# Block two's attention: a written TensorE order, raw queries and keys, one norm chain, compression between column tiles

## The chip, the core and the metric

One core of one Trainium2 chip runs the whole program. The metric is device time in microseconds, the median of several executions. TensorE does the matrix products, VectorE, ScalarE and GpSimd (POOL in the views) the elementwise work, and the SyncE queue (SP) issues the weight loads from HBM.

## What is computed

Two transformer blocks over 256 tokens of width 1024. The change is in the second. It normalises its input, projects it by one wide matrix and runs three branches: a sparse attention (NSA) with a compressed, a selected and a window part, a causal depthwise convolution of 31 taps, and an attention over a memory of 256 tokens. Each branch has an output product and a sigmoid gate of 1024 columns; their sum goes through another product, and a feed-forward layer follows.

```python
def hybrid_layer(x, mem, ...):
    proj = rms_norm_2(x, norm_mix) @ w_in
    q_nsa, kv_nsa, g_nsa, conv_in, q_mem, g_merge = split(proj)
    q = rms_norm_2(heads(q_nsa, 8), nsa_qk_norm[0])             # 8 heads of 64, 2 groups
    kc = rms_norm_2(compress_blocks(k_c, ...), nsa_qk_norm[1])  # gelu(blocks @ w1) @ w2
    vc = compress_blocks(v_c, ...)
    ks, kw = rms_norm_2(k_s, nsa_qk_norm[2]), rms_norm_2(k_w, nsa_qk_norm[3])
    o_nsa = gates of three softmax attentions: (kc, vc), (ks, v_s), (kw, v_w)
    u = a * sigmoid(ag)                                         # conv_in = a, ag
    br_conv = silu(layer_norm(conv31(u))) @ w_conv_out
    o_m = softmax(rms_norm(q_mem) @ rms_norm(km).T) @ vm        # 4 heads of 128
    merged = gm0 * (o_nsa @ w_nsa_out) + gm1 * br_conv + gm2 * (o_m @ w_mem_out)
    h = x + merged @ w_out
    ...
```

## The kernel before, in words

Activations lie with features on partitions and 256 tokens along the free axis. Big products take each fp32 weight tile as a high and a low half (fp32r): `Stream.prepare` loads 128x1024 fp32 (512 KB) into one of four `raw` buffers (L492), ScalarE writes the high half (L495) and VectorE, or POOL for the tiles listed in `pool`, the low half (L499); there are three buffers for each half. `gemm_b` then does, for each column tile of 128 columns and 8 slices of depth, 24 products: high by high (L318), high by low (L320), low by high (L322). Two column tiles share a PSUM bank, and an evacuation follows (L1039 for heads and convolution inputs, L1073 for gates).

`block_two` runs: the first 8 column tiles of `w2a` (compressed, selected and window keys, queries), a narrow product for the branch gates, the values (`w2v`, L358), the next 8 tiles (the convolution's two inputs), `compress` (chunks of `wc1`, L1174, loaded into eight of the 27 big tiles; a fold, L1180; the gelu; second products L1198 and L1213; a norm, L1203), the last 4 tiles (memory queries), then `nsa` and `mem_attention`. `head_norms` (L990 to L1001) takes squares, sums over the head by products (L996) and a chain of some twelve small VectorE steps (L371 to L377); it runs once for queries, once for keys and once for memory queries. Key norms are spread by products with the identity (L1231) and multiplied into the keys. In `nsa`, compressed scores (L1258) go through a softmax over 16 columns (L1260 to L1274) and are transposed (L1277); for each of eight heads `first(n)` makes scores (L1292), mask and maximum (L1298), exponentials (L1305) and the scaling by one over the sum and the gate (L1312, on POOL); `second(n)` transposes (L1324), copies (L1327) and multiplies by the values (L1334, L1335), adds the compressed part (L1337) and splits the result ("on", L416 and L417). A memory head does scores (L1362), maximum (L1364), exponentials (L1368), scaling (L1373), transposes (L1375), values (L1380) and the split ("om").

The program text gives each engine's instructions priorities, and a scheduler with its own model of costs turns them into a fixed order for each engine; weight loads and evacuations are raised. Only dependencies and this scheduler set TensorE's order. The 24 gate tiles (`w2g`) come after attention in the text, and the scheduler uses them to fill TensorE between attention's steps. The convolution's 124 taps (L1392, L1394) run on VectorE at low priority, followed by its norm (L1404 to L1427), which ends in "uc". After attention come three branch products, memory, NSA and convolution, in this order.

PSUM has eight banks: two "pj" for column tiles, three "pa", two "pb" for transposes and one "pc" for the heads' outputs.

Of the kernel before, what the change touches and what calls it, by code (L numbers as in the profile page):

```python
# [17 lines left out]
T = 256  # L18
# [54 lines left out]
def constants():  # L73
# [22 lines left out]
    c["half"] = (p[:, None] // 64 == np.arange(2)[None]).astype(f)  # L96
    c["mean64"] = (p[:, None] // 64 == p[None] // 64).astype(f) / 64
# [17 lines left out]
def layout(i):  # L115
# [22 lines left out]
    a["w2a"] = pack_b(np.concatenate([kc, vc, ks, kw, pairs(qn.T).T, cv[:, 512:], cv[:, :512], qm], 1))  # L138
# [44 lines left out]
class Kern:  # L183
# [90 lines left out]
    def gemm_b(self, st, kt, nts, x, evac, lead=None, order=None, single=0, joint=()):  # L274
# [10 lines left out]
        while i < nts:  # L285
            if i in joint:
# [8 lines left out]
                i += 1  # L295
                continue
            c = min(1 if i >= nts - single else 2, nts - i)
            ps = self.pj().rearrange("p (a t) -> p a t", a=2)
            if lead and i == 0:
# [9 lines left out]
                i += c  # L309
                continue  # L310
            for j in range(c):
                o, at = (i + j) * kt, 0
                while at < kt:
# [9 lines left out]
                    at = to  # L323
            with self.tc.high_priority(offset=50000):
                evac(i, c, ps[:, :c])
            i += c

# [36 lines left out]
    def rsqrt(self, v, n):  # L364

        nc = self.nc
        ti = self.gsmall("rs_i", [128, 16], I32)[:, :n]
        hv = self.gsmall("rs_h", [128, 16])[:, :n]
        t = self.gsmall("rs_t", [128, 16])[:, :n]
        y = self.gsmall("rs_y", [128, 16], bufs=4)[:, :n]  # L370
# [52 lines left out]
def nothing():  # L423
    pass

# [490 lines left out]
def between_norms(K, B):  # L916
# [16 lines left out]
    nc.vector.tensor_copy(rc, y[:, 2:])  # L933
    rr = K.to_row(rc, "rr")
# [70 lines left out]
def block_two(K, B, KM, vm, out):  # L1005
# [9 lines left out]
    kc2 = [K.small("kc2", [128, 2, 128], bufs=2) for _ in range(2)]  # L1015
    ksw = K.small("ksw", [128, 512], bufs=1)
    q = K.t4("q")
    gn = K.small("gn", [128, 256], bufs=1)
    ag, u = K.t4("ag"), K.small("u", [128, 4, 286], bufs=1)
    nc.gpsimd.memset(u[:, :, :30], 0.0)  # L1020
    qm = K.t4("qm")
    K.claim(q, ag, qm, *gm, cv, *ON.tiles, *OM.tiles)

    def ev(i, c, ps):
        if i == 0:
            for kv in range(2):
# [6 lines left out]
        d = {2: (ksw, 2), 4: (q, 4), 6: (q, 4), 8: (ag, 8), 10: (ag, 8), 12: None, 14: None, 16: (qm, 16),  # L1033
             18: (qm, 16)}[i]
        if d is None:
            o = u[:, i - 12:i - 10, 30:]
        else:
            o = d[0][:, (i - d[1]) * 256:(i - d[1] + 2) * 256].rearrange("p (a t) -> p a t", a=2)
        nc.vector.tensor_tensor(o, ps, bc(rr, 2), op=OP.mult)  # L1039
# [16 lines left out]
    pg = K.pt()[:, :48].rearrange("p (t n) -> p t n", t=2)  # L1056
    for t in range(2):
        mm(pg[:, t], lhsT=gn[:, t * 128:t * 128 + 128], rhs=con["fold"][:, :24], start=True, stop=True)
    gate = K.small("gate", [128, 2, 24], bufs=1)
    nc.scalar.activation(gate, pg, AF.Sigmoid)  # L1060
# [10 lines left out]
    def evg(i, c, ps):  # L1071
        d = gm[i // 4][:, (i % 4) * 256:(i % 4 + c) * 256]
        nc.vector.tensor_tensor(d.rearrange("p (a t) -> p a t", a=c), ps, bc(rr, c), op=OP.mult)  # L1073
# [146 lines left out]
def nsa(K, q, ksw, vsw, kcn, vcb, gate, ON, mem):  # L1220
# [94 lines left out]
    def second(n):  # L1315
# [13 lines left out]
        if g == 0:  # L1329
            S["po"] = K.pt("pc")[:, :256]  # L1330
# [135 lines left out]
```

## Time and profile before

| | |
|---|---|
| Median of 3 executions | 954.8 us (954.7 to 959.84) |
| The profiled execution | 954.86 us, span 953.1 us |
| Mean granted TensorE clock | 0.979 |
| TensorE, VectorE, ScalarE, POOL busy | 914.5, 691.0, 480.9, 143.0 us |

A span runs from the first to the last recorded instruction of the program. Busy time of an engine is the union of its instructions. PE is TensorE, DVE VectorE, ACT ScalarE. A releaser ("<-") is the instruction that ended a wait, and the granted clock (PEclk) is the share of 2.4 GHz that TensorE was given. Block two's first column tile begins at about 482 us of the span.

### The profile page before, as it was taken

To read this page: it belongs to the slowest core of one execution; us is meant where nothing else is said; L and a number is where in the kernel's file an instruction comes from. 1 tells how busy PE (TensorE), PEld (TensorE's weight loads), DVE (VectorE), ACT (ScalarE), POOL (GpSimd) and SP (SyncE) were. 2 spreads that over 40 slices of the span, in tenths; PEclk is the share of its full clock that TensorE was granted. 3 is DMA by queue.
4 is the path that set the end of the run, shared out by engine and by line. 5 is a ranking of instruction groups with operands and counts; after the bars stand their busy time and mean duration, and the time that the engine had idled before them with its cause. 6 is when DMAs were issued, how large, how long until landed. Compare 5 with 4: busy or idle time off the path is not lost. (4 is left out here: it accounts for less than half of the span.)

```text
span 953.1 us, 17109 instructions
## 1 busy us (share of the span) xinstructions
PE 914.5 (96%) x6816; PEld 838.0 (88%) x6816; DVE 691.0 (73%) x1169; ACT 480.9 (50%) x719; POOL 143.0 (15%) x167
## 2 busy tenths in 40 slices
PE   8988999999999999999999987799999999999998
PEld 6986789999999999888999887677799988888887
DVE  6698758857776665555666958989998878888653
ACT  5555665744555554444534221466754655555432
POOL 1022012200010000011210313453513100000000
PEclk9999999999999999999999967999999999999999
DMA  7634325665656666566675622322246556665672
GB/s 262 203 127 132 103 72 158 205 205 179 227 175 187 179 182 193 155 181 194 200 264 162 215 67 89 99 79 67 67 152 182 184 176 192 180 189 184 191 209 65
DMA packets 44287, 155.64 MB, mean 163 GB/s; under 512 B 5040, under 2 KB 6576, under 8 KB 44208
## 3 DMA queue, kind: packets, MB, share of 16 engines
q1 hardware_dynamic: 43776, 153.48, 52.3%
q8 instruction: 53, 0.87, 0.4%
q10 hardware_dynamic: 432, 1.08, 0.3%
q14 instruction: 26, 0.21, 0.1%
HBM read 153.49 MB, written 1.05 MB: 162 GB/s over the span
## 5 line engine op out<-in xcount | busy, mean ns | idle before, releaser
L495 ACT CAST hi<-raw 128x1024 fp32r<-128x1024 f32 x276 | 288.2, 1047 | 323.6 <-PE pj L320 159.3
L499 DVE TENSOR_TENSOR lo<-raw,hi 128x1024 fp32r<-128x1024 f32 x260 | 323.1, 1244 | 108.8 <-ACT hi L495 98.8
L291 PE MATMUL pj<-hid,hi 128*128 128x512 f32 x378 | 134.2, 399 | 0.0
L291 PE MATMUL pj<-xf,hi 128*128 128x512 f32 x320 | 113.2, 399 | 0.0
L292 PE MATMUL pj<-hid,lo 128*128 128x256 f32 x378 | 106.1, 281 | 0.0
L292 PE MATMUL pj<-xf,lo 128*128 128x256 f32 x320 | 89.8, 281 | 0.0
L291 PEld LDWEIGHTS pj<-hid,hi 128*128 128x128 f32 x378 | 71.0, 188 | 17.3
L448 POOL TENSOR_TENSOR acc<-acc,ffr 128x256 f32<-128x256 f32 (+1 forms) x25 | 27.4, 1103 | 311.3 <-ACT ffr L441 311.2
L291 PEld LDWEIGHTS pj<-xf,hi 128*128 128x128 f32 x320 | 60.1, 188 | 14.9
L292 PEld LDWEIGHTS pj<-hid,lo 128*128 128x128 f32 x378 | 71.4, 189 | 0.0
L1394 DVE SCALAR_TENSOR_TENSOR cv<-u,par,cv 128x256 f32<-128x256 f32 x120 | 69.9, 614 | 0.5
L292 PEld LDWEIGHTS pj<-xf,lo 128*128 128x128 f32 x320 | 60.4, 189 | 0.0
L499 POOL TENSOR_TENSOR lo<-raw,hi 128x512 fp32r<-128x512 f32 x32 | 44.2, 1403 | 68.3 <-ACT hi L495 54.6
L318 PE MATMUL pj<-xm,hi 128*128 128x256 f32 x336 | 52.0, 294 | 0.0
L320 PE MATMUL pj<-xm,hi 128*128 128x256 f32 x336 | 51.7, 292 | 0.0
L322 PE MATMUL pj<-xm,lo 128*128 128x256 f32 x336 | 51.3, 293 | 0.0
L318 PEld LDWEIGHTS pj<-xm,hi 128*128 128x128 f32 x336 | 46.6, 200 | 1.7 <-issue 0.7
L322 PEld LDWEIGHTS pj<-xm,lo 128*128 128x128 f32 x336 | 45.9, 199 | 0.8 <-issue 0.6
L320 PEld LDWEIGHTS pj<-xm,hi 128*128 128x128 f32 x336 | 45.9, 198 | 0.6 <-issue 0.4
L320 PE MATMUL pj<-xn,hi 128*128 128x256 f32 x304 | 44.2, 285 | 0.0
L322 PE MATMUL pj<-xn,lo 128*128 128x256 f32 x304 | 43.9, 284 | 0.0
L318 PE MATMUL pj<-xn,hi 128*128 128x256 f32 x304 | 43.5, 285 | 0.0
(456 smaller groups left out, 1746.1 us busy)
## 6 DMA issues: line engine op xcount, KB each, us to landing
raw<-in_wf_dram SPq DMA_DIRECT2D x64, 512.0 KB, 3.6
raw<-in_wgu_dram SPq DMA_DIRECT2D x44, 512.0 KB, 3.8
raw<-in_w1g_dram SPq DMA_DIRECT2D x24, 512.0 KB, 3.7
raw<-in_w2g_dram SPq DMA_DIRECT2D x24, 512.0 KB, 3.7
raw<-in_wdn_dram SPq DMA_DIRECT2D x22, 512.0 KB, 3.8
raw<-in_w2a_dram SPq DMA_DIRECT2D x20, 512.0 KB, 3.7
raw<-in_w1a_dram SPq DMA_DIRECT2D x16, 512.0 KB, 4.8
raw<-in_wo_dram SPq DMA_DIRECT2D x16, 512.0 KB, 4.0
```

The lines of the kernel that those rows point to most:

```text
L291: mm(ps, lhsT=st.hi(w), rhs=x.both(k), start=k == 0, stop=False, skip_group_check=True)
L292: mm(ps[:, :T], lhsT=st.lo(w), rhs=x.h(k), start=False, stop=k == kt - 1, skip_group_check=True)
L318: mm(ps[:, j], lhsT=st.hi(o + k), rhs=x.h(k), start=k == 0, stop=False)
L320: mm(ps[:, j], lhsT=st.hi(o + k), rhs=x.l(k), start=False, stop=False)
L322: mm(ps[:, j], lhsT=st.lo(o + k), rhs=x.h(k), start=False, stop=k == kt - 1)
L448: self.engine.tensor_tensor(a, a, s, op=OP.add)
L495: nc.scalar.copy(hi, raw)
L499: eng.tensor_tensor(lo[:, o:o + n], raw[:, o:o + n], hi[:, o:o + n].bitcast(F32), op=OP.subtract)
L1394: nc.vector.scalar_tensor_tensor(o, u[:, c, k:k + 256], w[:, c, k:k + 1], o, op0=OP.mult, op1=OP.add)
```

## The change

The convolution's columns become the first 8 of `w2a`; compressed, selected and window keys, queries and memory queries follow as 12 tiles. Queries, window and selected keys and memory queries are evacuated raw by ScalarE, without the token norm; one chain of sums and one reciprocal square root (32 columns) takes the place of three, with the token norm's epsilon carried into it (`B.eps`). `gemm_b` becomes a generator `steps_b` that yields after each column tile, and inside one block TensorE runs in the order of the text: compression goes chunk by chunk between column tiles, each chunk loaded into the ring of four `raw` buffers; gate tiles are called one by one between attention's steps (`fill(gates, 1)`); a memory head's scores, transposes and values stand a turn apart. The low halves of all gate tiles are VectorE's, probabilities are scaled by ScalarE (second half of the tokens) and VectorE (first half), POOL's products for the convolution's and the compression's inputs go to VectorE, and half of the second copies of the keys' low halves to ScalarE.

```diff
-    a["w2a"] = pack_b(np.concatenate([kc, vc, ks, kw, pairs(qn.T).T, cv[:, 512:], cv[:, :512], qm], 1))
+    a["w2a"] = pack_b(np.concatenate([cv[:, 512:], cv[:, :512], kc, vc, ks, kw, pairs(qn.T).T, qm], 1))
...
+def fill(steps, n):
+    for _ in range(n):
+        next(steps, None)
...
+        d, o = {2: (ksw, 0), 4: (q, 0), 6: (q, 512), 8: (qm, 0), 10: (qm, 512)}[i]
+        nc.scalar.copy(d[:, o:o + 512], ps.rearrange("p a t -> p (a t)"))
...
-    K.gemm_b(st, 8, 8, B.X, ev, lead=norms)
+    K.gemm_b(st, 8, 8, B.X, eva, lead=norms)
     K.wide = False
-    nc.vector.tensor_tensor(gn, K.gemm_n(K.narrow("wgn", B.gain), B.x), rr, op=OP.mult)
-    vsw = [K.small("vsw", [128, 256], bufs=2) for _ in range(2)]
+    s3 = nc.scalar.activation(ag, ag, AF.Sigmoid)
+    nc.vector.tensor_tensor(u[:, :, 30:], u[:, :, 30:], ag.rearrange("p (c t) -> p c t", c=4), op=OP.mult)
...
-    K.gemm_a(K.stream("w2v", 256), 8, 1, B.X, 256, evv)
-    K.gemm_b(_Shift(st, 64), 8, 8, B.X, lambda i, c, ps: ev(i + 8, c, ps))
...
-    kcn, vcb, s2 = compress(K, kc2)
-    s3 = nc.scalar.activation(ag, ag, AF.Sigmoid)
-    for j in range(4):
-        nc.gpsimd.tensor_tensor(u[:, j, 30:], u[:, j, 30:], ag[:, j * 256:j * 256 + 256], op=OP.mult)
-    K.gemm_b(_Shift(st, 128), 8, 4, B.X, lambda i, c, ps: ev(i + 16, c, ps))
-    with tc.issue_after(s3.ins), tc.issue_after(s2.ins):
-        mem = mem_attention(K, qm, KM, vm, OM)
-        last = nsa(K, q, ksw, vsw, kcn, vcb, gate, ON, mem)
...
-    K.gemm_b(K.stream("w2g", pool=[i for i in range(24) if i % 3]), 8, 24, B.X, evg)
+    with tc.manual_schedule(engines={mybir.EngineType.PE}):
+        heads = K.steps_b(_Shift(st, 64), 8, 12, B.X, evb)
+        fill(heads, 6)
+        cmp = compress(K, kc2, N)
+        for _ in range(6):
+            next(cmp)
+            fill(heads, 1)
+        next(cmp)
+        nc.vector.tensor_tensor(gn, K.gemm_n(K.narrow("wgn", B.gain), B.x), rr, op=OP.mult)
+        next(cmp)
+        K.gemm_a(K.stream("w2v", 256), 8, 1, B.X, 256, evv)
+        next(cmp)
+        pre = nsa_operands(K, N, B.eps)
+        next(pre)
...
+        gates = K.steps_b(K.stream("w2g"), 8, 24, B.X, evg)
+        fill(gates, 2)
+        next(cmp)
+        finish(pre)
+        fill(gates, 1)
+        finish(cmp)
+        with tc.issue_after(s3.ins), tc.issue_after(s4.ins), tc.issue_after(N.sig.ins):
+            last = nsa(K, N, ON, mem_attention(K, N, KM, vm, OM), gates)
+        finish(gates)
...
         for ch in range(4):
-            raw = K.t4("wc1")
-            nc.sync.dma_start(raw, K.a["wc1"][kv * 4 + ch])
-            raws.append(raw)
...
-        for o in range(0, 128, 32):
-            nc.vector.tensor_copy(part[o:o + 30, kv], pa[o:o + 30, kv])
+            with K.tc.high_priority(offset=100000):
+                raw = K.wp.tile([128, 1024], F32, tag="raw", name=K.nm("wc1"), bufs=4)
+                nc.sync.dma_start(raw, K.a["wc1"][kv * 4 + ch])
...
+            if 4 * kv + ch < 7:
+                yield
+    nc.scalar.copy(part, pa)
+    yield
...
-        for b in (1, 0):
-            for t in (1, 0):
-                nc.gpsimd.tensor_scalar(P[t][:, b], P[t][:, b], den[:, t, b:b + 1], 0.0, op0=OP.mult, op1=OP.add)
+        for b in range(2):
+            nc.scalar.mul(P[1][:, b], P[1][:, b], den[:, 1, b:b + 1])
+            nc.vector.tensor_scalar(P[0][:, b], P[0][:, b], den[:, 0, b:b + 1], None, op0=OP.mult)
...
+    fill(gates, 1)
     first(0)
+    fill(gates, 1)
+    scores()
     first(1)
-    for n in range(8):
-        if n < 6:
-            first(n + 2)
-        second(n)
-        if n % 2:
-            mem(n // 2)
+    fill(gates, 1)
+    m = None
+    for i in range(4):
+        turned(2 * i)
+        if m:
+            next(m)
+        if i == 3:
+            fill(gates, 1)
+            m2 = mem(i)
+            next(m2)
+        else:
+            first(2 * i + 2)
+        fill(gates, 1)
+        turned(2 * i + 1)
+        if i == 0:
+            compressed()
+        fill(gates, 1)
+        if i < 3:
+            first(2 * i + 3)
+        values(i)
+        if m:
+            finish(m)
+        fill(gates, 1)
+        if i < 3:
+            m = mem(i)
+            next(m)
+            fill(gates, 1)
+    next(m2)
+    fill(gates, 1)
+    finish(m2)
     return S["last"]
```

`turned(n)` holds a head's transposes and copies, `values(i)` the value products of a pair of heads with the compressed part and the split, `scores()` and `compressed()` the compressed softmax and its transposes. `mem(i)` yields after its scores and scaling and again after its transposes.

## Rows read from the trace of the kernel before

**Rows 1.** The page: busy time of each engine, its share, instructions.

```profile
PE 914.5 (96%) x6816; PEld 838.0 (88%) x6816; DVE 691.0 (73%) x1169; ACT 480.9 (50%) x719; POOL 143.0 (15%) x167
```

**Rows 2.** Stretches: length, busy us of each engine (instructions), clock, DMA share, GB/s.

```profile
482.00:540.00 58.00, 57.29 (x498) 53.74 (x498) 42.36 (x77) 21.66 (x25) 8.07 (x12) 1.00 0.65 210
...
540.00:703.20 163.20, 140.13 (x965) 126.09 (x965) 138.13 (x363) 78.24 (x156) 63.53 (x64) 0.90 0.27 86
...
703.20:726.60 23.40, 23.40 (x197) 23.29 (x196) 19.88 (x33) 12.35 (x18) 6.16 (x3) 1.00 0.56 175
...
482.00:717.40 235.40, 211.62 (x1579) 193.92 (x1579) 193.95 (x464) 108.91 (x194) 71.60 (x76) 0.93 0.38 122
...
660.00:680.00 20.00, 19.49 (x128) 15.97 (x127) 19.37 (x54) 14.10 (x35) 10.22 (x12) 1.00 0.16 54
...
480.00:500.00 20.00, 19.73 (x165) 19.37 (x164) 14.06 (x33) 8.05 (x10) 1.74 (x4) 1.00 0.72 251
```

**Rows 3.** TensorE's waits, 540 to 704 us: total, times, longest; four of eight.

```profile
PE pt L1277 <- DVE sc L1274: 7.0, 1, 7.0
PE pt L1231 <- DVE hn_y L1001: 6.3, 1, 6.3
PE pt L1198 <- DVE cmp_h L1191: 3.6, 1, 3.6
...
PE pt L1334 <- DVE om L417: 1.4, 1, 1.4
```

**Rows 4.** The three half-clock stretches, columns as in rows 2: first, and sum.

```profile
555.50:572.60 17.10, 17.10 (x95) 16.89 (x94) 5.13 (x32) 4.20 (x5) 0.26 (x1) 0.50 0.12 34
...
sum 34.20, PE 30.66 PEld 29.73 DVE 17.18 ACT 7.78 POOL 0.26; mean PE 10.22 PEld 9.91 DVE 5.73 ACT 2.59 POOL 0.09
```

**Rows 5.** Timeline: the convolution's last step, and the first product that reads it.

```profile
717.36 0.42 DVE L417 TENSOR_TENSOR uc<-cv,uc 128x256 fp32r<-128x256 f32 x1
...
726.69 0.64 PE L318 MATMUL pj<-uc,hi 128*128 128x256 f32 x4
```

**Rows 6.** The chain that ended last: start, us, eight products of a gate tile.

```profile
697.15 0.96 PE pj L318 x8
```

**Rows 7.** VectorE by line and shape, 482 to 717.4: count, busy, mean ns, idle before.

```profile
L1394 DVE SCALAR_TENSOR_TENSOR cv<-u,par,cv 128x256 f32<-128x256 f32 x120 | 69.9, 614 | 0.5
L499 DVE TENSOR_TENSOR lo<-raw,hi 128x1024 fp32r<-128x1024 f32 x34 | 41.4, 1220 | 11.2 <-ACT hi L495 6.8 <-PE pj L322 4.2
L1073 DVE TENSOR_TENSOR gm<-pj,rr 128x512 f32<-128x512 f32 x12 | 8.2, 686 | 6.3 <-PE pj L322 6.1
...
L1373 DVE TENSOR_SCALAR P<-P,denm 128x256 f32<-128x256 f32 x8 | 3.5, 469 | 0.0
L1176 DVE COPY P<-pt 30x256 f32<-30x256 f32 x8 | 3.4, 419 | 0.1
```

**Rows 8.** POOL by line and shape, the same stretch: the scalings of the probabilities.

```profile
L1312 POOL TENSOR_SCALAR P<-P,den 128x256 f32<-128x256 f32 x16 | 11.8, 737 | 27.2 <-DVE nb L1303 11.2 <-DVE den L1309 8.8 <-ACT P L1305 6.3
L1312 POOL TENSOR_SCALAR P<-P,den 128x128 f32<-128x128 f32 x16 | 8.1, 506 | 0.0
```

**Rows 9.** Timeline, start and us: taps beside a POOL instruction, and without one.

```profile
546.49 2.72 POOL L499 TENSOR_TENSOR lo<-raw,hi 128x512 fp32r<-128x512 f32 x2 [9.28 <-ACT hi L495]
546.67 2.81 DVE L1394 SCALAR_TENSOR_TENSOR cv<-u,par,cv 128x256 f32<-128x256 f32 x2
...
607.64 1.66 DVE L1394 SCALAR_TENSOR_TENSOR cv<-u,par,cv 128x256 f32<-128x256 f32 x4
```

**Rows 10.** Timeline: scores and transposes of the first head and of a memory head.

```profile
619.10 1.63 PE L1292 MATMUL pt<-ks,qs 128*128 128x256 f32 x4
...
628.40 0.88 PE L1324 MATMUL pt<-con,P 128*128 128x128 f32 x6 [0.67 <-POOL P L1312]
...
650.64 1.03 PE L1362 MATMUL pt<-km,qm 128*128 128x256 f32 x4
...
659.34 0.44 PE L1375 MATMUL pt<-con,P 128*128 128x128 f32 x2 [0.21 <-DVE P L1373]
```

More of the change, by code (lines that the diff above doesn't have):

```diff
@@ L424, in nothing, with finish @@
     pass
+def fill(steps, n):
+    for _ in range(n):
+        next(steps, None)
+def finish(steps):
+    for _ in steps:
+        pass
 class Squares:
@@ L1075, in block_two @@
-    K.gemm_b(K.stream("w2g", pool=[i for i in range(24) if i % 3]), 8, 24, B.X, evg)
+    with tc.manual_schedule(engines={mybir.EngineType.PE}):
[12 more added lines that the diff above has]
+        next(pre)
+        pg = K.pt()[:, :48].rearrange("p (t n) -> p t n", t=2)
+        for t in range(2):
+            mm(pg[:, t], lhsT=gn[:, t * 128:t * 128 + 128], rhs=con["fold"][:, :24], start=True, stop=True)
+        N.gate = K.small("gate", [128, 2, 24], bufs=1)
+        s4 = nc.scalar.activation(N.gate, pg, AF.Sigmoid)
+        gates = K.steps_b(K.stream("w2g"), 8, 24, B.X, evg)
[7 more added lines that the diff above has]
+        finish(gates)
@@ L1201, in compress @@
     nc.vector.tensor_tensor(k2, k1, k1, op=OP.mult)
+    pv = K.pt()[:, :64]
+    for i in range(4):
+        for m in range(2):
+            mm(pv[32 * i:32 * i + 32], lhsT=h5[:, 1, m], rhs=w2[:, 1, m], start=m == 0, stop=m == 1)
+    N.vcb = K.small("cmp_v", [128, 128], bufs=1)
+    nc.vector.tensor_tensor(N.vcb.rearrange("p (g d) -> p g d", g=2), bc(pv, 2),
+                            con["slot"].unsqueeze(2).to_broadcast([128, 2, 64]), op=OP.mult)
+    yield
     pn = K.pt()[:, :16]
@@ L1254, in nsa @@
     col = lambda x: x.unsqueeze(2).to_broadcast([128, 16, 16])
-    pc = K.pt()[:, :256].rearrange("p (a c) -> p a c", c=16)
-    for t in range(2):
-        for i in range(4):
-            mm(pc[:, 8 * t + 2 * i:8 * t + 2 * i + 2], lhsT=q4[:, i, t * 128:t * 128 + 128], rhs=kcn, start=True,
-               stop=True)
-    nc.vector.tensor_tensor(s3, pc, col(rq.rearrange("p t n -> p (t n)")), op=OP.mult)
-    add, one = (bc(con[n].rearrange("p (t c) -> p t c", t=2), 8, 2) for n in ("cmp_add", "cmp_one"))
@@ L1282, in nsa, with compressed @@
+    def compressed():
+        pT = K.pt()[:, :256]
+        for t in range(2):
+            nc.tensor.transpose(pT[:, t * 128:t * 128 + 128], s[:, t * 128:t * 128 + 128], K.ident)
+        nc.vector.tensor_copy(PcT, pT)
     cz = con["causal0"]
@@ L1336, in second, with values @@
-        if g:
-            mm(po, lhsT=vcb[32 * i:32 * i + 32], rhs=PcT[32 * i:32 * i + 32], start=False, stop=True,
-               skip_group_check=True)
-            K.split(ON.h(i), ON.l(i), po)
+            w = K.small("PT", [128, 384], bufs=4)
+            nc.scalar.copy(w, pt)
+            S[n].append(w)
+    def values(i):
+        po = K.pt("pc")[:, :256]
+        PT = [S.pop(2 * i + g) for g in range(2)]
+        for b in range(2):
+            for t in range(2):
+                for g in range(2):
+                    vs = slice(b * 128 + g * 64, b * 128 + g * 64 + 64)
+                    mm(po[g * 64:g * 64 + 64, t * 128:], lhsT=vsw[t][:, vs],
+                       rhs=PT[g][b][:, 256:] if t else PT[g][b][:, :256], start=b + t == 0, stop=False,
+                       skip_group_check=True)
+        mm(po, lhsT=vcb[32 * i:32 * i + 32], rhs=PcT[32 * i:32 * i + 32], start=False, stop=True,
+           skip_group_check=True)
+        K.split(ON.h(i), ON.l(i), po)
@@ L1341, in nsa @@
+    fill(gates, 1)
     first(0)
+    fill(gates, 1)
+    scores()
     first(1)
[L1343 to L1348 removed]
+    fill(gates, 1)
+    m = None
+    for i in range(4):
+        turned(2 * i)
[5 more added lines that the diff above has]
+            next(m2)
+        else:
+            first(2 * i + 2)
[14 more added lines that the diff above has]
+            fill(gates, 1)
```

219 lines of the change are left out of this document (117 added, 102 removed).

## The prediction

> **What bounds the kernel now.** I read the page first. TensorE is busy for 96% of the span [rows 1], so a gain has to come out of its few per cent of idle time, or out of time in which it runs at half clock. The table by stage finds both in one place: from 482 to 540 us TensorE is full at full clock, from 540 to 703.2 it is busy 140.13 of 163.2 us at a mean granted clock of 0.90, and after 703.2 it is full again [rows 2]. That stretch is block two's attention, with the gate columns (w2g) as filler.
>
> Idle there is 163.20 - 140.13 = 23.1 us. The table of waits names it: the transposes of the compressed scores waited 7.0 us for VectorE, the broadcast of the key norms 6.3, the second compression product 3.6; with five smaller ones they add up to 23.0 [rows 3]. The clock is the second loss. Three stretches (34.2 us in all) were granted 0.50, that is 1.2 GHz, and TensorE was busy 30.66 us in them [rows 4]; the first follows the 3.6 us wait, the third the 7.0 us wait. At full clock that work takes half: 15.3 us lost.
>
> So the stretch can give back at most 23.1 + 15.3 = 38.4 us, since no edit removes a matrix product. The sum is made against the profiled execution: span 953.1, 954.86 with the 1.8 us around it, against a median of 954.8. Floor: 953.1 - 38.4 = 914.7 of span.
>
> VectorE is the other engine to watch: busy 193.95 of 235.40 us, 82%, from 482 until the convolution's result is ready at 717.8 [rows 2, 5]. The output product that reads it starts at 726.7, so there are 9 us of slack [rows 5].
>
> **The change part by part.** *Conv columns first.* They were tiles 8 to 15 of w2a and become 0 to 7. A tile is 24 products, 8 in 0.96 us [rows 6], so 2.88 us; the taps may start 8 x 2.88 = 23 us earlier. It costs TensorE nothing and gives VectorE a lower-priority reserve that fills its gaps.
>
> *Compression between column tiles, norms in one chain.* The 3.6 us wait gets the value columns (w2v, 48 products, 5.8 us by the same row), the sums of squares and two gate tiles in front of it. The 6.3 us wait was three rsqrt chains one after another behind half-clock sums; now one chain runs under two gate tiles (5.8 us). The 7.0 us wait was the compressed softmax; now it has the first two heads' work and two gate tiles, about 9 us, in front. I take all three as gone, and with them the half clock, which only appeared around them.
>
> *Weights of the compression through the ring of four.* Where chunks alternate with tiles, two loads of 512 KB are due per 2.88 us and a little: up to 364 GB/s. The most the trace shows is 251 GB/s at a DMA share of 0.72 [rows 2]. Six rounds are 6.3 MB, 25 us at that rate against 17.3 of tiles: 8 us short at worst, nothing if the share can rise or if ring and split tiles have run ahead. From 540 us on the share was only 0.27 [rows 2], so there is room to recover, and three split tiles stand ahead of TensorE; I take 1, ends 0 and 8. Behind a late chunk on SP's queue stand the next column tile, then w2v and the gate tiles, and TensorE, in written order, waits for each.
>
> *Work moved to VectorE and ScalarE.* 16 gate tiles lose POOL for their low halves: 16 x 1.220 = 19.5 us more on VectorE [rows 7]. Half of the 32 probability scalings come from POOL (0.737 and 0.506 us each [rows 8]) to VectorE: 16 narrow ones at about half of the 0.469 of L1373, 4 us; ScalarE takes the other 16 and the five evacuations of raw queries and keys; it is busy 108.91 of 235.40 us [rows 2], which hides them (if a head waits on one, that is in the heads' prices below). Off VectorE go eight copies of the compression (3.4 us, L1176) and five evacuations, each like L1073's 0.686: 3.4 us. Taken alone that is +16.7 us. But POOL's instructions block VectorE's: beside a POOL low half two taps took 2.81 us, with no POOL four took 1.66, 0.415 each [rows 9]. The 120 taps' 69.9 us [rows 7] become 49.8: -20. Other two-input forms (some 80 us of the rest) I let win a tenth, an estimate from the taps: -8. VectorE's bill to the convolution's end goes from 194 to about 183, or 191 without that tenth. So taking POOL away pays for itself.
>
> *Written order in the heads.* Each iteration of a head pair holds four gate tiles (11.5 us) and about 9 us of attention. New waits:
> - The first heads. Before, the first head needed 628.40 - 619.10 = 9.3 us from scores to transposes, with POOL's scaling inside [rows 10]. The written order puts two tiles (5.8), the compressed scores and the second head's scores (some 2.5) between, about 8.3 us. With the first keys and the compressed softmax I take 3 us; ends 0 and 8.
> - Memory heads a turn later. From scores to transposes a memory head needed 659.34 - 650.64 = 8.7 us [rows 10], in an order that did not hurry it. Written, only a gate tile (2.88) and one head's six transposes (0.7) lie between, 3.6 us, three times: 0 to 3 x 5.1 = 15 us. Without POOL in VectorE's way the chain is nearer the short end: 4 us.
> - One bank for outputs. `values(i)` and `finish(m)` follow each other on the only "pc" bank, three times, so the second waits for the copy and subtraction of the first; behind it on TensorE stands a gate tile, and VectorE waits for that one's evacuation. The wait stands in the trace once: 1.4 us [rows 3]. 3 x 1.4 = 4.2; ends 3 x 1 and 3 x 3.
>
> The Trainium skill (Perfetto Trace Analysis, Matmuls) speaks against this part: independent groups should rotate through PSUM banks so that emptying one overlaps the next. Taken for each of the eight uses of this bank it would cost 8 x 1.4 = 11.2 us, a sum of 938; the trace shows one such wait for eight uses, since a tile usually lay between.
>
> *What is late next.* Gates end at 703.2 - 38.4 + 12.2 = 677. The two products before the convolution's take 726.7 - 703.2 = 23.5 us, so its result is due at 700.5, 218 us after 482. At before's 82%, VectorE's 183 us end at 705, at 88% at 690: I take a stall of 2.5 us, ends 0 and 15 (191 us at 82%).
>
> Sum: 38.4 - (1 + 3 + 4 + 4.2 + 2.5) = 23.7 us gained; 953.1 - 23.7 + 1.8 = **931 us**.
>
> **The rivals.**
> - *VectorE ends late* (17 in 100). Its other forms win nothing: 191 us at 82% end at 715, a stall of 15 instead of 2.5: 943. For it: VectorE was busy 19.37 of 20 us from 660 to 680 [rows 2], and two products' halves and evacuations join there. Against: 20 us of taps can move into gaps that start 23 us earlier.
> - *The waits only move* (10 in 100). In a written order TensorE has nothing else to issue; if half of the three long waits stay (8.5 us) and half the half clock with them (7.7), 16 of the 38 us are not won: 947. For: a VectorE that stands in order behind an attention step serves the next one late. Against: each chain has 6 us or more in front.
> - *Slower* (7 in 100). The taps are not slow because of POOL. Then they stay at 69.9 us and VectorE has 194 + 16.7 = 211 us to do; at 82% that ends at 739 against 700: 38 us of stall, 967. It decides from about 209 us on, where the stall is 36 and the time passes 964. Against it stand the pairs of taps with and without POOL [rows 9].
> - *Nearly all of it* (7 in 100). The lower ends hold, 3 us for the bank and nothing else: 953.1 - 38.4 + 3 + 1.8 = 919.5.
>
> **How the numbers follow.** 920 to 940 has 59 in 100, its likeliest value 931. The range reaches from the last rival, rounded down to 919, over the first to the second, 947. One per cent, about what a measurement here can tell, is 945.3 and 964.4. Faster: 59 + 7 + 11 of the 17 = 77. Slower: 7. Within: 16.
>
> **What would show it.** Right: no granted 0.50 between 540 and the gates' end; no wait of TensorE over 3 us there; taps near 0.47 us each in the trace; POOL nearly empty; three waits of about 1.4 us for the "on" subtraction; gates ending near 677. Wrong: TensorE waiting for "uc" before the last branch product (first rival), taps at 0.6 with POOL idle (third), long waits with half clock behind them (second), waits of the compression's products for their loads (the ring).

## The result

The changed kernel took 944.72 us (median of 4 runs, 942.96 to 948.07), the kernel before beside it 955.55: a ratio of 0.9905 [0.9877, 0.9933]. A second measurement of the two gave 0.9893 [0.9875, 0.9911]. The forecast gain was 24 us; it is 10 to 11. The profiled execution has a span of 946.3 us, 6.8 less than before.

The page's busy line, against [rows 1]:

```profile
PE 907.4 (96%) x6816; PEld 834.7 (88%) x6816; DVE 675.7 (71%) x1167; ACT 495.6 (52%) x745; POOL 69.7 (7%) x94
```

The stretch of block two's attention: the kernel before, then the changed one, each from its first column tile to the end of its gate columns (columns as in [rows 2]).

```profile
482.00:703.20 221.20, 197.43 (x1461) 179.83 (x1461) 180.49 (x439) 99.90 (x181) 71.60 (x76) 0.92 0.37 118
```

```profile
482.00:540.00 58.00, 57.73 (x493) 53.82 (x497) 50.91 (x107) 22.54 (x26) 0.00 (x0) 1.00 0.62 196
540.00:696.60 156.60, 132.93 (x971) 123.62 (x964) 113.29 (x327) 92.27 (x181) 0.00 (x0) 0.89 0.34 106
sum 214.60, PE 190.66 PEld 177.44 DVE 164.20 ACT 114.80 POOL 0.00; mean PE 95.33 PEld 88.72 DVE 82.10 ACT 57.40 POOL 0.00
```

The stretch is 6.6 us shorter, yet TensorE is idle in it as long as before: 221.20 - 197.43 = 23.8 us, then 214.60 - 190.66 = 23.9. These are its waits in the changed kernel (total, times, longest), against [rows 3]:

```profile
PE pt L1476 <- DVE P L1471: 7.3, 3, 2.7
PE pt L1329 <- DVE cmp_kn L1260: 5.1, 1, 5.1
PE pj L368 <- ACT hi L519: 3.7, 1, 3.7
PE pt L1482 <- DVE on L431: 3.4, 3, 1.6
PE pt L1291 <- DVE hn_y L391: 2.4, 1, 2.4
PE pj L368 <- DVE glow L1094: 1.3, 1, 1.3
PE pt L1393 <- ACT P L1382: 0.4, 1, 0.4
```

Of the three long waits of before two are gone and the key norms' broadcast (`hn_y`) is down from 6.3 to 2.4. In their place stand waits of a memory head's transposes, of the compressed scores (`cmp_kn` is the compressed keys with their norm), of the value columns (w2v, two rows) and of a memory head's products. The half clock came back too. Four of the changed kernel's seven stretches at 0.50, and the sum of all seven, against [rows 4]:

```profile
546.50:549.90 3.40, 2.99 (x14) 2.99 (x15) 3.40 (x5) 2.91 (x4) 0.00 (x0) 0.50 0.62 167
556.80:567.00 10.20, 10.20 (x50) 10.20 (x50) 2.69 (x14) 1.31 (x3) 0.00 (x0) 0.50 0.13 48
...
590.90:597.70 6.80, 6.66 (x29) 6.46 (x30) 4.75 (x23) 1.39 (x4) 0.00 (x0) 0.50 0.01 2
...
645.50:648.90 3.40, 3.40 (x17) 3.30 (x16) 3.24 (x15) 1.38 (x5) 0.00 (x0) 0.50 0.18 72
...
sum 34.00, PE 33.44 PEld 32.63 DVE 20.12 ACT 11.94 POOL 0.00; mean PE 4.78 PEld 4.66 DVE 2.87 ACT 1.71 POOL 0.00
```

So 33.44 / 2 = 16.7 us are lost to the clock, against 15.3. What shrank is the work itself: busy time less half of that at half clock was 197.43 - 15.33 = 182.1 us and is 190.66 - 16.72 = 173.9, 8.2 us less. (A second profile of the changed kernel, read from its own first column tile, at 484.1, to the end of its gate columns, gives 173.9 too.) One group carries most of it, the value products `pt<-PT,vsw`. Their own busy time before, then after:

```profile
630.00:690.00 60.00, 12.38 (x64) 7.23 (x64) 0.00 (x0) 1.00 0.23 71
```

```profile
600.00:690.00 90.00, 6.10 (x64) 4.00 (x64) 0.00 (x0) 0.94 0.30 94
```

The same 64 products take half the time, 6.3 of the 8.2 us. Before, the eight of one head took 1.5 us. Now the sixteen of two heads do, since consecutive ones write different halves of the output's partitions:

```profile
630.93 1.52 PE L1407 MATMUL pt<-PT,vsw 128*64 128x256 f32 x16
```

The Trainium skill has this rule (TensorEngine Tiling (Array Packing), Tiling Modes): products of 64 columns leave the array two tiles, and different tiles can load weights and multiply at the same time. This trace agrees: records of a pair start 6 to 7 ns apart.

### The profile page after: what moved, and what is told of

Same layout as the page of the kernel before. It is cut to its first block, busy times and chain, and to the rows that moved or that the text cites. A ratio compares the mean times of both kernels' runs of the same rounds, so it can differ in the third digit from the quotient of the medians.

```text
span 946.3 us, 17011 instructions
## 1 busy us (share of the span) xinstructions
PE 907.4 (96%) x6816; PEld 834.7 (88%) x6816; DVE 675.7 (71%) x1167; ACT 495.6 (52%) x745; POOL 69.7 (7%) x94
## 4 chain that ended last, share of the span: by engine, by line
PE 85%; DVE 6%; ACT 4%; DMA 2%; issue 2%; POOL 1%; SPq 0%; DVEq 0%; ACTq 0%; POOLq 0%
PE pj L296 17%; PE pj L325 15%; PE pj L327 14%; PE pj L329 14%; PE pj L297 9%; PE pj L368 5%; DVE lo L523 2%; ACT hi L519 2%; PE pj L310 1%; PE pj L311 1%; PE pj L309 1%; DVE cv L1496 1%; DMA raw<-in_w2a_dram 1%; POOL lev L782 1%; PE pt L1276 1%
## 5 line engine op out<-in xcount | busy, mean ns | idle before, releaser
L523 DVE TENSOR_TENSOR lo<-raw,hi 128x1024 fp32r<-128x1024 f32 x276 | 343.0, 1244 | 116.7 <-ACT hi L519 110.7
L325 PEld LDWEIGHTS pj<-xm,hi 128*128 128x128 f32 x336 | 48.5, 209 | 4.2 <-issue 2.7
L1496 DVE SCALAR_TENSOR_TENSOR cv<-u,par,cv 128x256 f32<-128x256 f32 x120 | 51.5, 477 | 0.0
L329 PE MATMUL pj<-xm,lo 128*128 128x256 f32 x336 | 47.9, 286 | 0.0
L327 PEld LDWEIGHTS pj<-xm,hi 128*128 128x128 f32 x336 | 46.2, 204 | 0.0
L329 PEld LDWEIGHTS pj<-xn,lo 128*128 128x128 f32 x304 | 39.5, 192 | 0.5 <-issue 0.4
```

The lines of the kernel that those rows point to most:

```text
L325: mm(ps[:, j], lhsT=st.hi(o + k), rhs=x.h(k), start=k == 0, stop=False)
L327: mm(ps[:, j], lhsT=st.hi(o + k), rhs=x.l(k), start=False, stop=False)
L329: mm(ps[:, j], lhsT=st.lo(o + k), rhs=x.h(k), start=False, stop=k == kt - 1)
L523: eng.tensor_tensor(lo[:, o:o + n], raw[:, o:o + n], hi[:, o:o + n].bitcast(F32), op=OP.subtract)
L1496: nc.vector.scalar_tensor_tensor(o, u[:, c, k:k + 256], w[:, c, k:k + 1], o, op0=OP.mult, op1=OP.add)
```

## The experiments

**The theory and its rivals.** After the result I read it so: the waits moved because the written order has too little in front of six short chains, each wait costs more than its length because the clock falls behind it, and the gain is the value products' alone. The rivals: VectorE is late whatever the order; the saved work is only in the records; the clock falls for another reason. The ratios below are to the kernel before as measured beside each run (its medians were 953.0 to 956.5 us), and idle and half clock are TensorE's in the stretch of block two's attention (busy time at half clock; half of it is lost). Each stretch goes from the first product of its first column tile, which stands between 480.7 and 484.2 us in these profiles, to the first product of the branch that follows the gates. Where that start differs, spans differ by up to 3.5 us ahead of any edit, so the stretch says more than the span.

| kernel | ratio [95%] | median us | stretch | idle | busy at half clock |
|---|---|---|---|---|---|
| before | 1 | 954.8 | 221.2 | 23.8 | 30.6 |
| changed | 0.9905 [0.9877, 0.9933] | 944.7 | 214.6 | 23.9 | 33.6 |
| after_again | 0.9893 [0.9875, 0.9911] | 946.2 | 212.2 | 21.4 | 33.8 |
| values_by_head | 0.9901 [0.9884, 0.9919] | 946.8 | 212.0 | 20.0 | 30.3 |
| before_values | 1.0071 [1.0043, 1.0098] | 960.4 | 226.5 | 32.4 | 33.9 |
| norms_first | 0.9834 [0.9804, 0.9863] | 939.8 | 209.7 | 20.6 | 29.5 |
| scalings_on_pool | 0.9924 [0.9896, 0.9953] | 947.2 | 214.3 | 23.6 | 33.7 |
| halves_on_pool | 1.0036 [1.0010, 1.0062] | 957.0 | 225.0 | 29.7 | 42.8 |
| memory_later | 0.9715 [0.9699, 0.9731] | 929.2 | 197.7 | 11.7 | 23.8 |
| later_values_apart | 0.9809 [0.9767, 0.9851] | 935.8 | 201.4 | 11.2 | 19.8 |
| later_chunks_own | 0.9706 [0.9678, 0.9735] | 926.3 | 192.8 | 10.1 | 16.9 |
| later_sums_apart | 0.9689 [0.9653, 0.9725] | 924.6 | 190.9 | 9.6 | 14.1 |
| later_sums_norms | 0.9611 [0.9580, 0.9641] | 916.9 | 182.3 | 5.6 | 3.4 |
| all_moved | 0.9579 [0.9552, 0.9606] | 913.7 | 181.3 | 4.0 | 3.4 |
| quiet_values_by_head | 0.9592 [0.9567, 0.9616] | 916.4 | 183.4 | 3.2 | 3.4 |
| quiet_memory_early | 0.9678 [0.9649, 0.9708] | 924.0 | 189.9 | 11.1 | 6.3 |
| quiet_halves_on_pool | 0.9816 [0.9794, 0.9838] | 937.7 | 204.9 | 17.9 | 21.6 |

**The yardstick, after_again.** No edit.

> The changed kernel once more, as the yardstick of the other runs on this chip. Both theories: 0.988 to 0.993 of the kernel before, about 944 us. In the stretch from the first column tile behind the convolution's columns to the end of the gate tiles: some 215 us, of them 24 us idle on TensorE and some 17 us lost to the half clock.

**A memory head's turns later, memory_later.** One gate tile more, and the next head's scores, stand in front of a memory head's transposes, and one gate tile in front of its products; nothing else moves.

```diff
         turned(2 * i)
-        if m:
-            next(m)
...
         fill(gates, 1)
+        if m:
+            next(m)
         turned(2 * i + 1)
...
         values(i)
+        fill(gates, 1)
         if m:
             finish(m)
-        fill(gates, 1)
```

> A memory head's transposes go behind one more gate tile, and its products behind the gate tile that follows the value products. Theory that each of these waits is paid twice, in idle time and in the half clock behind it: the waits of 7.3 us (transposes) and 3.4 us (products) fall below 1 us together, the three half-clock stretches of 3.4 us at 621, 645 and 669 us are gone (5 us), 12 to 16 us less: 929 to 933 us. Rival that VectorE is late anyway and the wait moves to the next instruction that needs it (heads' transposes, value products, the gate tiles' banks): idle time and half clock of that stretch stay within 4 us, the time is 941 to 945 us.

The waits it was aimed at are gone from the list, those in front of them are unchanged against after_again, and one of 0.9 us for a copy of transposed weights (`PT`) is new:

```profile
PE pt L1329 <- DVE cmp_kn L1260: 5.2, 1, 5.2
PE pt L1291 <- DVE hn_y L391: 2.4, 1, 2.4
PE pj L368 <- DVE glow L1094: 1.5, 1, 1.5
PE pj L368 <- ACT hi L519: 1.1, 1, 1.1
PE pt L1407 <- ACT PT L1396: 0.9, 1, 0.9
```

From 600 us on the clock stays full:

```profile
540.00:600.00 60.00, 49.83 (x349) 48.10 (x342) 43.87 (x135) 27.95 (x49) 0.00 (x0) 0.80 0.37 113
600.00:678.50 78.50, 77.22 (x604) 70.92 (x603) 67.65 (x193) 63.28 (x132) 0.00 (x0) 1.00 0.39 119
```

Against after_again that is 9.7 us less idle and 10 / 2 = 5 us less lost to the clock, a stretch 14.5 us shorter, and 17 us less time in the median. The theory holds: two gate tiles per memory head in the wrong place cost more than the whole change had brought. VectorE was not late; it was asked too early.

**The norm chains ahead of VectorE's other work, norms_first.** The priority of the two chains is raised; TensorE's order stays.

```diff
+    with K.tc.high_priority(offset=200000):
         nc.vector.tensor_scalar(k2, pn, EPS, None, op0=OP.add)
         y = K.rsqrt(k2, 16)
...
+    with K.tc.high_priority(offset=200000):
...
         K.rsqrt(v, 32, y)
```

> The two short chains of VectorE on which TensorE waits (the norm chain of the 32 columns, the norm chain of the compressed keys) go ahead of VectorE's other ready work. Theory that they are late because VectorE takes other work between their steps: the chain of the compressed keys takes 3 to 5 us instead of 11.4, the waits of 5.1 us (scores) and 2.4 us (key norms) fall below 1 us together, the half-clock stretches at 573.8 and 590.9 us (5.1 us lost) are gone, 9 to 12 us less: 933 to 936 us. Rival that the chains are bound by their own latency: the waits stay above 5 us together, the time within 2 us of 944.7 us.

The wait for the 32 columns' norm went, that for `cmp_kn` fell from 5.2 to 2.5 us, and two new ones came (1.5 for the head's weights, 1.2 for the split keys): 6 us gained in the median instead of 9 to 12. (The profiled execution was the slowest of the four; its stretch is only 2.5 us shorter, with 3.1 us of wait at the value columns instead of 1.0.) The chain itself hardly shrank. Its first and last step in the changed kernel:

```profile
579.41 0.17 DVE L1256 TENSOR_SCALAR cmp_k<-pt 128x16 f32<-128x16 f32 x1 [1.41 <-PE pt L1255]
...
590.80 0.19 DVE L1260 TENSOR_TENSOR cmp_kn<-cmp_k,con 128x32 f32<-128x32 f32 x1
```

and here, 10.4 us instead of 11.6, only 4 us earlier:

```profile
575.39 0.17 DVE L1258 TENSOR_SCALAR cmp_k<-pt 128x16 f32<-128x16 f32 x1 [0.66 <-PE pt L1255]
...
585.58 0.18 DVE L1261 TENSOR_TENSOR cmp_kn<-cmp_k,con 128x32 f32<-128x32 f32 x1
```

Expecting 3 to 5 us for the chain was wrong. Its fifteen own steps are busy for 2.6 us in both kernels; in the rest VectorE mostly does other work, low halves of 1.2 us above all, which still stands between them in its planned order. So the raised priority did not clear its way, and what the chain would take undisturbed was not measured. What helped is to start it earlier, as later_sums_norms shows.

**The sums of squares apart, later_sums_apart.** On memory_later: keys', queries' and memory queries' sums are issued at three places between wide products, not in one block of 40 (their PSUM bank becomes "pc" for it).

```diff
         at += n * m
+        if m == 2:
+            yield
...
-        for _ in range(6):
+        pre = nsa_operands(K, N, B.eps)
+        for k in range(6):
             next(cmp)
+            if k in (1, 4):
+                next(pre)
             fill(heads, 1)
```

> The version with the memory heads later, with the one- and two-column sums of squares in three groups (8, 16 and 16 products) between wide products: keys' and queries' between the chunk turns, the memory queries' where all stood. Theory that the clock falls behind the narrow products themselves, with no wait ahead of them: the half-clock stretch of 10.2 us at 553 us shrinks to one of 3.4 us or to none, 3 to 5 us less: 924 to 926 us. Rival that it falls because of the wait for the value columns' halves just before (2.6 us here): the stretch stays at 10 us, the time within 1.5 us of 929.

Busy time at half clock fell by 9.7 us, idle by 2.1, the stretch by 6.8, the median by 4.6 (the ratio by 0.0026, and the intervals overlap). The wait at the value columns went as well, since 24 sums now stand in front of it, so this run alone does not tell the narrow products from the wait. The next one does.

**The compression's chunks out of the ring, later_chunks_own.** On memory_later, each chunk in a buffer of its own.

```diff
-                raw = K.wp.tile([128, 1024], F32, tag="raw", name=K.nm("wc1"), bufs=4)
+                raw = K.t4("wc1")
```

> The version with the memory heads later, with the compression's eight chunks in buffers of their own instead of the stream's ring of four raw buffers. Theory that the ring holds back the value columns' chunk: the wait at the value columns (2.6 us in that version, and a half-clock stretch of 3.4 us behind it) falls below 0.5 us, 3 to 5 us less: 924 to 926 us. Rival that the DMA traffic of those 20 us (share 0.7) holds it back, whichever buffer it goes to: the wait stays between 1.5 and 4 us, the time within 2 us of 929.

The ring was the cause: of 2.6 us of waits at the value columns 0.3 are left and the stretch is 4.9 us shorter (the ratio, 0.9706 against 0.9715, can't resolve that). It bears on the narrow products too: with no wait in front but one of 0.27 us at 543.2, the 40 sums ran at full clock from 549.76, and the clock fell all the same, behind them and before any other wait.

```profile
549.76 4.70 PE L1276 MATMUL pt<-con,hsq 128*128 128x2 f32 x40
```

```profile
554.10:561.00 6.90, 6.90 (x34) 6.90 (x34) 3.03 (x15) 1.57 (x3) 0.00 (x0) 0.51 0.00 0
```

**The norms started earlier, later_sums_norms.** On later_sums_apart: the second compression products and the keys' mean product come one gate tile earlier each (not two, as the expectation has it for the latter), with the 32 columns' chain at raised priority.

```diff
-        fill(gates, 2)
+        fill(gates, 1)
         next(cmp)
+        fill(gates, 1)
+        finish(cmp)
         finish(pre)
         fill(gates, 1)
-        finish(cmp)
```

> The version with the memory heads later and the sums of squares apart, with two more moves for what still waits there (5.2 us for the compressed keys' norm, 2.9 us for the norm of the 32 columns, and the two half-clock stretches behind them, 17 us with some 7 us lost): the compressed keys' mean product goes two gate tiles further ahead of the scores, and the norm of the 32 columns goes ahead of VectorE's other ready work. Theory that each wait is paid twice and goes when its work starts earlier: both waits below 1.5 us together, less than 4 us busy at the half clock, 10 to 14 us less: 911 to 915 us. Rival that the waits move on to the heads' operands or maxima behind them: 3 to 6 us of new waits there, the half clock stays above 8 us, 918 to 923 us.

The scores wait no more: the chain runs from 563.07 to 573.70, still 10.6 us, and they start at 573.85. New waits are 2.7 us for the first head's weights and 1.7 for its keys. The gain is 7.7 us, between the theory and the rival: idle moved on in part, the half clock did not.

**What was left, all_moved.** On later_sums_norms: chunks in their own buffers, and one gate tile from behind the first value products to ahead of the first head's transposes.

> The best version so far (0.9611) with two more moves: the compression's chunks in buffers of their own, and one gate tile moved from behind the first value products to ahead of the first head's transposes, which wait 2.7 us there. Theory that what is left is these waits alone: the 2.7 us are gone, the chunks give nothing more (no wait at the value columns is left in that version), idle time of the stretch 3 us instead of 5.6, 2 to 4 us less: about 914 us. Rival that the moved tile is missed where it stood, and the wait moves to the first memory head's scores or the second pair's transposes: within 1 us of 917.

913.7 us, 0.9579 [0.9552, 0.9606]: the best version, some 40 us faster than the kernel before, 31 faster than the changed one. 4.0 us idle and 1.7 us of half clock are left in the stretch. That the last two moves gained is likely, not shown: the stretch is 1.0 us shorter than in later_sums_norms, and the intervals overlap.

**The order of the value products.** Four runs bear on it. values_by_head undoes the turns in the changed kernel, quiet_values_by_head in all_moved:

```diff
-        for b in range(2):
-            for t in range(2):
-                for g in range(2):
+        for g in range(2):
+            for b in range(2):
+                for t in range(2):
```

later_values_apart (on memory_later) sets the two heads a gate tile apart:

```diff
             compressed()
+        values(i, 0)
         fill(gates, 1)
...
-        values(i)
+        values(i, 1)
```

before_values gives the kernel before the turns, in `second`, at the pair's second head (the copies of transposed weights get other buffers for it, the memory heads' a single one of their own):

```diff
-        if g == 0:
-            S["po"] = K.pt("pc")[:, :256]
...
         if g:
+            po = K.pt("pc")[:, :256]
+            for b in range(2):
+                for t in range(2):
+                    for j in range(2):
...
```

> The value products go head by head again (all of one head's, then the other's) instead of taking turns between the two halves of the output's partitions; all else as in the changed kernel. Theory that the saved work is the two heads' products running side by side on TensorE: the group pt<-PT,vsw is busy 11 to 12 us instead of 5.8, the span is 5 to 6 us longer, the time about 950 us, 0.996 of the kernel before. Rival that the smaller busy time is only a matter of when the records begin and end, and the gain lies in the waits: busy time changes in the records or not, the time stays within 1.5 us of 944.7 us.

> The version with the memory heads later (0.9715), with the value products of a pair's two heads a gate tile apart, as far from each other as in the kernel before. Theory of running side by side: busy 11.7 us instead of 5.8, and with no half clock and no wait near them the stretch and the time grow by all of it, 5 to 6 us: 934 to 935 us, against 929.2. Rival: 0 to 1 us.

> The kernel before with one part of the change alone: a pair of heads' value products is issued together, taking turns between the two halves of the output's partitions (the transposed weights of the first head are held for it in a fourth buffer). Theory that the work saved on TensorE is the two heads running side by side: the group pt<-PT,vsw is busy 5.8 us instead of 11.7, the time is 4 to 6 us less, 0.994 to 0.996 of the kernel before. Rival that the products only start together in the records, and each pair takes as long as two: the start of the next work behind a pair moves by nothing, ratio 0.999 to 1.001.

> The best version (0.9579, 4 us idle and 3.4 us of half clock in the stretch), with the value products head by head. Theory that the turns between the two halves save what the records show: the group is busy 8.9 us instead of some 6.5, nothing near it can take that up, 2 to 3 us more: ratio 0.960 to 0.961. Rival that the order within a pair is worth nothing to the time: 0.957 to 0.9585.

Busy time of the group in values_by_head, later_values_apart and before_values:

```profile
600.00:690.00 90.00, 8.88 (x64) 6.48 (x64) 0.00 (x0) 0.94 0.29 93
```

```profile
600.00:684.00 84.00, 12.11 (x64) 7.66 (x64) 0.00 (x0) 1.00 0.34 107
```

```profile
630.00:700.00 70.00, 7.36 (x64) 4.40 (x64) 0.00 (x0) 0.99 0.25 76
```

Apart, the products take what they took before (12.11 us, against 6.72 in memory_later), and the time grows by 6.6 us, TensorE's work in the stretch (busy less half of that at half clock) by 6.1, the stretch by 3.7, since half clock takes 2.0 us less: the saving is real. One head right behind the other saves over half of it already (8.88, not 12.38), since the second head's first products start while the first head's last still run. The 2.8 us between that and the turns show nothing in the changed kernel, where idle and half clock happened to shrink by as much (21.4 to 20.0, and 33.8 to 30.3). With the turns undone in all_moved, the median is 2.7 us longer, the stretch 2.1, but the intervals overlap: likely, not shown. And in the kernel before the saving brings a loss. There the work in the stretch fell by 4.8 us and idle grew by 8.6:

```profile
PE pt L1324 <- POOL P L1312: 8.8, 7, 1.9
```

With the first head's value products gone from between the transposes, TensorE reached the next ones before POOL's scalings were done (1.3 us of such waits before).

**POOL.** scalings_on_pool puts the four scalings of a head back on POOL in the changed kernel; halves_on_pool puts 16 gate chunks' low halves there, quiet_halves_on_pool the same in all_moved.

```diff
-        gates = K.steps_b(K.stream("w2g"), 8, 24, B.X, evg)
+        gates = K.steps_b(K.stream("w2g", pool=[i for i in range(24) if i % 3]), 8, 24, B.X, evg)
```

> The changed kernel with the four scalings of each head's weights back on POOL, as before, and the streams' low halves left on VectorE. Theory that POOL's place in a head's chain costs more than the work it takes off ScalarE and VectorE (four scalings one after the other, 0.74 us each, before TensorE can transpose): waits of the heads' transposes grow from 0.4 us to 4 us or more, the taps from 0.48 to 0.53 us, the time 4 to 12 us longer, 949 to 957 us. Rival that the gate tiles between hide it: within 2 us of 945.

> The changed kernel with the low halves of the gate stream back on POOL for 16 of its 24 chunks, as before. Theory that taking POOL away paid for itself on VectorE and that neither engine sets the end: the taps go back from 0.48 to about 0.6 us each (beside POOL's 737 ns subtractions), VectorE loses some 13 us of low halves and gains 15 us of taps, the time stays within 2 us of 945. Rival that VectorE's free time is what the changed kernel lives on: the waits for VectorE (7.3, 5.2, 3.4 us) grow by over 3 us together, 949 us or more.

> The best version with the low halves of 16 gate chunks on POOL. Theory that POOL costs only where it shifts an in-order queue behind which TensorE waits: with gate tiles in front of each use the waits grow by less than 4 us, 0 to 6 us more, 0.958 to 0.964. Rival that POOL's halves are slow in themselves (a half takes 1.3 us on POOL, two a chunk, 2.6 us against a gate half tile of 2.9 us, so TensorE comes to wait for them) or slow VectorE's steps beside them by the 5 to 25 per cent of the taps: over 8 us more, 0.967 or above.

The scalings' place is worth nothing that can be told (0.9924 against 0.9893), as the rival had it: 1.8 us of waits for POOL came. The halves' place is worth 12 us in the changed kernel and 24 in all_moved, so both theories failed, and the times lie where the rivals had put them (949 or more, over 8 us more). In the changed kernel the three waits for VectorE grew together by 6.8 us (22.7 against 15.9), which is what that rival named. In neither does TensorE wait for a low half, so half of the other rival falls; its other half is borne out: the taps take 553 ns in quiet_halves_on_pool against 476 in all_moved, 8.9 us in all. There TensorE waits for ScalarE's and VectorE's small steps:

```profile
PE pt L1413 <- ACT PT L1402: 6.4, 3, 3.4
PE pt L1335 <- DVE cmp_kn L1263: 5.1, 1, 5.1
PE pt L1489 <- DVE on L431: 2.2, 1, 2.2
```

Nor is VectorE full: 117.15 of 145.60 us from 540. With the halves elsewhere, the order of ScalarE's and VectorE's instructions, which isn't written but planned, came out different. In halves_on_pool, for one, the output's copy on ScalarE (642.35) stands behind four exponentials, and a memory head's products wait 4.05 us for it:

```profile
643.25 2.08 PE L1482 MATMUL pt<-PTm,vm 128*128 128x256 f32 x4 [4.05 <-DVE on L431]
```

How much of the 24 us is order, how much POOL's own pace (1.3 us for half a chunk) and how much VectorE's slower steps beside it no run tells apart: the orders of the other two engines were not written out.

**A wait's price, quiet_memory_early.** all_moved, with a memory head's transposes where the changed kernel has them.

> The best version with the memory heads' transposes back where the changed kernel has them, right behind the next head's six transposes; their products stay a gate tile later. Theory that each of the three waits costs more than its length: waits of 7 to 8 us come back, and with them three half-clock stretches of 3.4 us, 5 us lost, 12 to 13 us more: 0.970 to 0.972. Rival that the clock falls only where several waits come close together, as in the changed kernel: 7 to 8 us more, 0.965 to 0.967.

8.2 us of waits came back, idle grew by 7.1 us, half clock by 2.9 busy, the time by 10.2 us, the span by 8.6: nearer the rival. (all_moved's one stretch at half clock, behind the sums, didn't appear here.) The first two waits left the clock full; the third, of 3.82 us, was followed by a fall.

```profile
600.42 0.63 PE L1483 MATMUL pt<-con,P 128*128 128x128 f32 x4 [2.27 <-DVE P L1478]
621.25 0.70 PE L1483 MATMUL pt<-con,P 128*128 128x128 f32 x4 [1.98 <-DVE P L1478]
643.99 0.69 PE L1483 MATMUL pt<-con,P 128*128 128x128 f32 x2 [3.82 <-DVE P L1478]
```

```profile
643.60:650.40 6.80, 6.24 (x28) 5.84 (x29) 1.92 (x6) 5.99 (x7) 0.00 (x0) 0.50 0.10 39
600.00:643.50 43.50, 37.76 (x292) 34.34 (x292) 42.59 (x131) 31.38 (x73) 0.00 (x0) 1.00 0.34 103
```

In the changed kernel each of the three such waits, 2.47, 2.10 and 2.69 us, was followed by a stretch at 0.50. Ahead of the second and third stood a wait of 0.92 us for the output bank, 10 and 11 us before; ahead of the first there was none for 16 us:

```profile
621.05 0.63 PE L1476 MATMUL pt<-con,P 128*128 128x128 f32 x4 [2.47 <-DVE P L1471]
...
644.50 0.70 PE L1476 MATMUL pt<-con,P 128*128 128x128 f32 x4 [2.10 <-DVE P L1471]
```

So "each wait is paid twice" holds for the changed kernel and not in general, and neither a wait's length nor a second one near it tells the cases apart. What does stays open.

## Why the forecast was wrong

**Right: where the loss lies, and that it can be had.** 38.4 us were said to be recoverable in this stretch. all_moved has a span of 913.1 us, 40.0 less than before, with 5.7 us still lost and 6.6 us of work saved.

**Wrong: "I take all three as gone, and with them the half clock".** Two went, the third shrank. But the tiles I counted as their cover are in an order that now makes TensorE ask early for other things. I had priced the ring, the first heads, the memory heads and the bank at 12.2 us in all, none of them with half clock behind it; the scores' own operand, and what was left of the key norms, at nothing. 23.9 us of waits and 16.7 of half clock came; with the stall for `uc` the forecast left 14.7 for everything.

**Wrong: "no edit removes a matrix product".** True of the count, wrong as a floor: the order removed 8.2 us of TensorE's time. Only this error made up for part of the other, and that was luck: without it the stretch would have come out no shorter than before.

Term by term:

| term | forecast (ends) | changed kernel |
|---|---|---|
| chunks in the ring | 1 (0 to 8) | 5.0 of waits (2.5 in the second profile), 1.5 of clock behind them |
| first heads | 3 (0 to 8) | 0.4 |
| scores for the keys' norm | not priced | 5.1, and 3.3 of clock |
| key norms | gone | 2.4, and 1.7 of clock |
| memory heads | 4 (0 to 15) | 7.3, and 5.1 of clock |
| one bank for outputs | 4.2 (3 to 9) | 3.4 |
| narrow sums | no cost | 5.1 of clock (3.4 in later_chunks_own, almost without the ring's waits) |
| stall for `uc` | 2.5 (0 to 15) | 0 |

The mechanisms of the ring, the memory heads and the bank were right, with sizes inside their ends; for the memory heads the row of 8.7 us [rows 10] against 3.6 us in front had said 5.1 each, and I leaned to the short end for want of POOL. The keys' norm is the one I passed over. I gave the 7.0 us wait of the compressed softmax 9 us of cover and did not ask what the softmax itself starts from: a chain of 11.6 us on VectorE, begun two gate tiles and a head's scores, 6.5 us, ahead of it. The narrow sums I took as cover for others, though I had called them "half-clock sums" myself.

**Right: VectorE.** The taps take 477 ns each, forecast 0.47, and POOL is empty from 482 to 696.6 us.

```profile
L1496 DVE SCALAR_TENSOR_TENSOR cv<-u,par,cv 128x256 f32<-128x256 f32 x120 | 51.5, 477 | 0.0
```

The convolution's result is ready at 711.7, 8 us before its product at 719.99. VectorE is not the bound, so the first and the third rival fell. That taking POOL away "pays for itself" was too weak: leaving the halves on POOL costs 12 us, though little of it through the taps (499 ns in halves_on_pool), which I had given as the reason.

**The rivals.** "The waits only move" described the mechanism, at 10 in 100; I let half of the waits stay, and as much as all came back. Its 947 was near the time because the work saved, which no case held, paid for the rest. Against it I had set that each chain has 6 us or more in front. That is the step that failed: the cover was not compared with what each chain takes. For the memory heads my own price list had 3.6 us in front and 8.7 needed (6.7 to 7.3 in the changed kernel, from scores to transposes); for the keys' norm, with 6.5 in front, I had looked up no length, and it took 11.6.

**The signs named beforehand.** Gates end at 696.6, not 677; granted 0.50 appears seven times; waits of 5.1 and 3.7 us exceed the 3 I had named. Taps, POOL and the three waits for "on" (3.4 us, forecast 4.2) came as said.

## What to carry to other kernels

Where an engine's order is written by hand, write beside each request the length of the chain behind it, from its last input to its result, and the work that stands in front; a chain longer than that work is a wait, and raised priority took only 1.2 us off the 11.6 here. Putting two gate tiles in front of such requests gained more (17 us in the median) than the whole rearrangement. And before calling an engine's work fixed, look at products that use half of its columns: two of them for different halves cost the time of one, if they follow each other.

## What the runs showed of the hardware

- Products of 64 columns overlap across heads also without turns, where one head's end meets the next one's start (8.88 us, against 6.10 in turns); a gate tile between them undoes it (12.11).
- Behind a run of 40 one- and two-column products the granted clock fell to 0.50 with 0.27 us of waiting in front (later_chunks_own). Of the three groups of 8, 16 and 16 between wide products, the last was followed by a fall in four profiles of six, with no wait shortly before it (all_moved, at 553.7), though by a shorter one: 3.4 us busy at half clock instead of 6.8.
- Waits of 2.73 us (later_sums_norms, at 582), 2.27 and 1.98 us (quiet_memory_early) left the clock at 1.00. In the changed kernel waits of 2.10, 2.47 and 2.69 us did not. The Trainium skill (TensorE: Matmul & The Clock Gate, A second HAM failure mode: psum-queue depth-cycling) says that frequent short idles between groups of products make the clock go back and forth; the changed kernel, with eleven waits and seven falls in the stretch, agrees, and no run here settles how many are too many.
